# A decoder layer on one core: the feed-forward's first product as seven half-size products per block

## The chip, the core and the metric

The kernel runs on one core of a Trainium2 chip. Its time is the device time of one execution in microseconds (us), the median of several runs. The core has TensorE (matmuls; PE in the rows, PEld for its weight loads), VectorE (DVE), ScalarE (ACT), GpSimd (POOL) and SyncE (SP, which here only issues DMAs). Each engine works off its own queue in order. Matmuls write to PSUM, eight banks of 128 x 512 float32; everything else lies in SBUF.

## What is computed

One layer of a decoder on 512 tokens with 1024 features: a mixer with three groups of heads, then a feed-forward, each between two norms. The change touches the feed-forward:

```python
h = rmsnorm(x, pre_ffn_g[l])
gate, up = jnp.split(h @ w_ffn_in[l], 2, axis=-1)
f = (jax.nn.silu(gate) * up) @ w_ffn_out[l]            # 2816 -> 1024
x = x + rmsnorm(f, post_ffn_g[l])
```

All arrays are float32. D_FF is 2816, which is 22 blocks of 128.

## The kernel before

Every float32 operand of a large product is split into a high part (`h`, rounded to float32r by ScalarE) and a low part (`l`, the rest, by VectorE or GpSimd), and a product is three float32r matmuls: high x high, high x low, low x high. Weights arrive by DMA in pieces of 512 KB into the tile `wf` (pool `wpool`, two buffers); `Feed.split` (lines 174 to 186) makes `wh` (line 183, ScalarE) and `wl` (line 185, VectorE, or GpSimd where `on_pool` says so) from them. All matmuls are issued on line 112, transposes on line 117, weight loads by DMA on line 156.

The stages that matter here, in order:

- The mixer's output product (`tm_gemm`, two halves of 512 features). Its second half goes token tile by token tile; behind each tile come the epilogue (lines 1113 to 1132) and `turn` (lines 1141 to 1162): the norm, transposes of the tile to channels-first into the banks `rb` and `yb`, and the split into `h2` (line 1158, ScalarE) and `l2` (line 1159, VectorE), both 128 x 8 x 512.
- The first product of the feed-forward (lines 1171 to 1209). Blocks 0 and 1 are taken in two token halves of 256, so that the first half can start before the last tokens are turned: four weights (gate and up of two blocks), 24 matmuls of 256 columns each, then the second half. Blocks 2 to 21 follow with 512 columns: for gate and for up, eight slices of 128 features by three matmuls, 48 matmuls a block, in two banks `acc` or two banks `sb` in turn.
- `gate` (lines 1178 to 1183) of each block: silu on ScalarE into `etmp`, the product with up on VectorE, the high part (1182, ScalarE) and the low part (1183, VectorE).
- The second product (lines 1211 to 1219): `f_units`, pairs of blocks, each times 4 token tiles, in two halves of 512 features, with weights from `w_ffn_out` in the same manner.

The order of TensorE's instructions is written out by hand; `Order` (`od`) interleaves side work, such as the transposes of `turn`, by nominal times. For the other engines and their DMA queues a scheduler chooses the order when the kernel is built, by readiness in its own model and by priority; `tc.high_priority` raises it. An engine then executes that order as it stands. Synchronisation is derived from which tiles an instruction reads and writes.

SBUF is managed in pools on two stacks (`side="right"` is the second). A pool that is opened where a closed pool lay shares its memory. A pool opened with `reuse_waits="tile"` waits for the old tiles that it overlaps, one by one; without it the default "pool" holds. Line 1052 closes the pool `sol` (with the tile `y`) and line 1053 opens `early` there (`x2`, `grow`, `frow`); lines 1068 to 1072 close the mixer's pools and open `wsplit2` and `res`.

Of the kernel before, what the change touches and what calls it, by code (L numbers as in the profile page):

```python
# [96 lines left out]
def block_kernel(ctx: ExitStack, tc: tile.TileContext, x, pre_mix_g, w_in, rwkv_mu, rwkv_w0, rwkv_w2,  # L97
# [30 lines left out]
    def acc():  # L128
        return bank("acc", 2)
# [919 lines left out]
    for ui, unit in enumerate(o_units):  # L1049
        if ui == 2:  # L1050
            od.until("att2")
            sol.close()
            early = ph2.enter_context(tc.tile_pool(name="early", bufs=1, side="right"))
            x2 = early.tile([128, NB, D], F32, name="x2")
            grow = early.tile([128, D], F32, name="grow")
            frow = early.tile([128, D], F32, name="frow")
            act.dma_start(grow, brow(post_mix_g[0], D))
            act.dma_start(frow, brow(pre_ffn_g[0], D))
# [9 lines left out]
    ph1.close()  # L1068
    wsp2 = ph2.enter_context(tc.tile_pool(name="wsplit2", bufs=2, side="right"))


    res = ph2.enter_context(tc.tile_pool(name="res", bufs=1))
    wpools = (wspool, wsp2)
    h2 = res.tile([128, KB, S], F32R, name="h2")
    l2 = res.tile([128, KB, S], F32R, name="l2")
    sm = res.tile([128, 3 * NB], F32, name="sm")
    raw = res.tile([128, NB, 512], F32, name="raw")

    def tm_gemm(fd, ah, al, units, fin, by_token, banks, halves=(0, 1), parts=1):


        for hf in halves:
# [20 lines left out]
            for t in range(NB):  # L1103
                for part in range(len(pa[t])):
                    for ui in range(nun - tail, nun):
                        step(ui, t, part)

    def epilogue(gr, after):
        ys = {}

        def fin(t, p, a, b):
# [3 lines left out]
            if a == 0:  # L1115
                ys[t] = raw[:, t, :]
            elif a == 512:
                ys[t] = res.tile([128, 512], F32, name="etmp", bufs=2)
            dve.tensor_tensor(ys[t][:, a % 512:a % 512 + b - a], p, gr[:, a:b], op=OP.mult)  # L1119
# [21 lines left out]
    def turn(t):  # L1141
# [11 lines left out]
        for i in range(2):  # L1153
# [16 lines left out]

    FM = FB - KB
    fhm = res.tile([128, FM, S], F32R, name="fhm")
    flm = res.tile([128, FM, S], F32R, name="flm")
    fh = [fhm[:, i] if i < FM else mh[:, i - FM] for i in range(FB)]
    fl = [flm[:, i] if i < FM else ml[:, i - FM] for i in range(FB)]
    ffeed = Feed([(w_ffn_in[0], slice(0, 8), c + 128 * b, 128) for b in range(FB) for c in (0, FF)], wpools, on_pool=(1, 3))

    def gate(b, pg):
        f = res.tile([128, S], F32, name="etmp", bufs=2)
        act.activation(f, pg[0], AF.Silu)  # L1180
        dve.tensor_tensor(f, f, pg[1], op=OP.mult)
        act.copy(fh[b], f)
# [11 lines left out]

    ws = [ffn_w() for _ in range(4)]
# [5 lines left out]
    gate(0, pf[0:2])  # L1201
    gate(1, pf[2:4])
# [9 lines left out]
    orow = early.tile([128, D], F32, name="grow")  # L1212
    act.dma_start(orow, brow(post_ffn_g[0], D))
    wfeed = Feed([(w_ffn_out[0], pair_slice(k), 512 * hf, 512) for hf in range(2) for k in f_units], wpools)

# [34 lines left out]
```

## Time and profile before

| | us |
|---|---|
| median of 3 runs | 693.94 |
| lowest, highest | 693.78, 695.75 |
| the profiled execution, its own time | 693.72 |
| its span, first to last instruction | 692.0 |
| TensorE busy in it | 661.3 (96%) |
| VectorE, ScalarE, GpSimd busy | 335.6, 253.1, 137.0 |
| mean granted TensorE clock | 0.991 of full speed |

All rows come from that one profiled execution; times in them count from the span's start. The profiled end of a matmul is modelled, and matmuls overlap, so the pace of TensorE is read from starts of one matmul to starts of the next, not from durations.

### The profile page before, as it was taken

What the parts mean: (1) busy time and instruction counts of PE and PEld (TensorE: products, weight loads), DVE (VectorE), ACT (ScalarE), POOL (GpSimd) and SP (SyncE); (2) the same over time, 40 slices, a digit from 0 to 9 for tenths busy, and PEclk for the clock granted to TensorE, in tenths of its full rate; (3) what the DMA queues carried; (4) which work ended last, traced back from release to release, by engine and by line L of the source; (5) the groups of instructions that cost most, each with busy time, mean ns of one, the idle gap of its engine ahead of it and who ended that gap; (6) DMA issues with size and microseconds to landing.
All of it is one profiled execution on the core that took longest, in us unless ns stands there. A gap on an engine that the chain in (4) does not pass through costs nothing.

```text
span 692.0 us, 9733 instructions
## 1 busy us (share of the span) xinstructions
PE 661.3 (96%) x3918; PEld 542.8 (78%) x3918; DVE 335.6 (48%) x588; ACT 253.1 (37%) x451; POOL 137.0 (20%) x157
## 2 busy tenths in 40 slices
PE   7997999799999997997999999999999999999996
PEld 6876768677778885777988888888888888888885
DVE  4698879935354676358433233332323332222214
ACT  6753443435454463434422233222223221122111
POOL 6373447532423235115000000000000000000001
PEclk9999999899999999999999999999999999999999
DMA  7422112311212117225233333333333222323303
GB/s 234 121 62 62 33 38 82 92 32 37 50 31 60 33 55 251 94 59 152 68 116 101 105 99 92 91 92 95 109 100 91 92 91 92 94 99 101 99 4 122
DMA packets 80287, 61.15 MB, mean 88 GB/s; under 512 B 2121, under 2 KB 70129, under 8 KB 80241
## 3 DMA queue, kind: packets, MB, share of 16 engines
q1 hardware_dynamic: 78192, 57.70, 27.3%
q10 hardware_dynamic: 2048, 2.82, 1.4%
q8 instruction: 31, 0.51, 0.3%
q14 instruction: 16, 0.12, 0.1%
HBM read 58.41 MB, written 2.10 MB: 87 GB/s over the span
## 4 chain that ended last, share of the span: by engine, by line
PE 51%; DVE 2%; issue 1%; ACT 1%; POOL 1%; DVEq 0%; POOLq 0%; ACTq 0%
PE sb L112 21%; PE acc L112 21%; PE yb L112 3%; PE rb L112 3%; PE ob L112 2%; DVE x L1132 1%; DVE xs L1149 1%; ACT raw L1145 1%; POOL rs L1129 0%; POOL ss L1147 0%; DVE etmp L1119 0%; ACT wdad L1113 0%; DVE wl L185 0%; DVEq L1246 0%; PE rb L117 0%
## 5 line engine op out<-in xcount | busy, mean ns | idle before, releaser
L183 ACT ACTIVATE wh<-wf 128x1024 fp32r<-128x1024 f32 (+2 forms) x120 | 104.1, 886 | 285.4 <-PE sb L112 123.1
L185 DVE TENSOR_TENSOR wl<-wf,wh 128x1024 fp32r<-128x1024 f32 (+1 forms) x76 | 89.3, 1180 | 170.7 <-ACT wh L183 168.4
L185 POOL TENSOR_TENSOR wl<-wf,wh 128x512 fp32r<-128x512 f32 (+2 forms) x44 | 71.4, 1641 | 102.8 <-ACT wh L183 70.6
L1129 POOL TENSOR_TENSOR rs<-rs,mhalf 128x1 f32<-128x1 f32 x8 | 6.2, 778 | 379.9 <-DVE rs L1124 376.2
L112 PE MATMUL acc<-l,wh 128*128 128x512 f32 (+1 forms) x192 | 71.7, 374 | 1.9 <-DVE l L1159 1.9
L112 PE MATMUL sb<-l,wh 128*128 128x512 f32 (+1 forms) x192 | 71.6, 373 | 0.0
L112 PE MATMUL sb<-h,wh 128*128 128x512 f32 (+1 forms) x192 | 71.5, 373 | 0.0
L112 PE MATMUL acc<-h,wh 128*128 128x512 f32 (+1 forms) x192 | 71.5, 372 | 0.0
L112 PE MATMUL sb<-h,wl 128*128 128x512 f32 (+1 forms) x192 | 71.1, 371 | 0.0
L112 PE MATMUL acc<-h,wl 128*128 128x512 f32 (+1 forms) x192 | 71.1, 370 | 0.0
L112 PE MATMUL acc<-bigh,wh 128*128 128x512 f32 (+1 forms) x168 | 68.3, 410 | 0.7 <-ACT bigh L276 0.5
L112 PE MATMUL acc<-bigl,wh 128*128 128x512 f32 (+1 forms) x168 | 64.0, 386 | 0.3
L112 PE MATMUL acc<-bigh,wl 128*128 128x512 f32 (+1 forms) x168 | 59.5, 379 | 0.0
L112 PEld LDWEIGHTS acc<-l,wh 128*128 128x128 f32 x192 | 36.1, 188 | 8.3 <-DVE l L1159 2.2
L112 PEld LDWEIGHTS acc<-h,wh 128*128 128x128 f32 x192 | 36.1, 188 | 6.6
L112 PEld LDWEIGHTS sb<-h,wh 128*128 128x128 f32 x192 | 36.1, 188 | 6.6
L112 PEld LDWEIGHTS acc<-h,wl 128*128 128x128 f32 x192 | 36.1, 188 | 6.5
L112 PEld LDWEIGHTS sb<-h,wl 128*128 128x128 f32 x192 | 36.1, 188 | 6.5
L112 PEld LDWEIGHTS sb<-l,wh 128*128 128x128 f32 x192 | 36.1, 188 | 6.1
L112 PEld LDWEIGHTS acc<-bigh,wh 128*128 128x128 f32 x168 | 32.0, 191 | 8.6 <-issue 2.0
L112 PEld LDWEIGHTS acc<-bigl,wh 128*128 128x128 f32 x168 | 32.1, 191 | 5.8 <-DVE bigl L277 0.9
L112 PEld LDWEIGHTS acc<-bigh,wl 128*128 128x128 f32 x168 | 30.2, 191 | 6.3
(345 smaller groups left out, 1271.0 us busy)
## 6 DMA issues: line engine op xcount, KB each, us to landing
wf<-in_w_ffn_in_dram SPq DMA_DIRECT2D x44, 512.0 KB
wf<-in_w_ffn_out_dram SPq DMA_DIRECT2D x22, 512.0 KB
wf<-in_w_in_dram SPq DMA_DIRECT2D x21, 512.0 KB
wf<-in_w_out_dram SPq DMA_DIRECT2D x8, 512.0 KB
xt<-in_x_dram SPq DMA_DIRECT2D x4, 512.0 KB
x<-in_x_dram SPq DMA_DIRECT2D x4, 512.0 KB
out_dram<-x SPq DMA_DIRECT2D x8, 256.0 KB
wf<-in_w_in_dram SPq DMA_DIRECT2D x4, 384.0 KB
```

Source lines behind the costliest of these rows:

```text
L112: return nc.tensor.matmul(out_, lhsT, rhs, **kw)
L183: act.activation(h[:, c], t[:, c], AF.Copy)
L185: eng.tensor_tensor(l[:, c], t[:, c], h[:, c].bitcast(F32), op=OP.subtract)
L1129: pool.tensor_tensor(r, r, mhalf[:, 0:1], op=OP.pow)
L1132: dve.scalar_tensor_tensor(x2[:, t, c:d], src, r, x2[:, t, c:d], op0=OP.mult, op1=OP.add)
L1145: act.activation(raw[:, t, :].bitcast(BF), x2[:, t, :], AF.Square, scale=1.0 / 32, accum_out=ss[:, t:t + 1])
L1149: dve.scalar_tensor_tensor(xs, x2[:, t, :], ss[:, t:t + 1], frow, op0=OP.mult, op1=OP.mult)
```

## The change

Blocks 0 and 1 of the first product stay as they were. For blocks 2 to 21 the product of the 256 x 1024 weights (gate and up, 128 columns each) with the 1024 x 512 tokens is cut in two in each direction: weights into a11, a12 (gate, features 0 to 511 and 512 to 1023) and a21, a22 (up), tokens into b11, b12, b21, b22 (features by token halves). Seven products of the half size replace eight, as in Strassen's method in Winograd's form: four sums of weights (s1 to s4) and four of tokens (t1 to t4) go in, and the results are combined afterwards.

- Sums of tokens: `turn` also writes `ht`, a float32 copy of the turned tokens (one more ScalarE copy per bank). VectorE forms t1 to t4 there once (four operations of 1024 elements), and each is split into high and low parts; t1 takes the place of the original quarter in `h2`, `l2`.
- Sums of weights, per block (`weights`): SP loads a21 into half of `sa`, a11 into half of `sc`, a11 and a12 into `g` (pool `wpool`), a22. GpSimd's queue then issues two accumulating loads of 256 KB: a22 is added onto a21 in `sa` (s1), a21 onto a11 in `sc` (s3). VectorE forms s2 = s1 + a11 into the other half of `sa` and s4 = a12 + s2 into the other half of `sc`. All are split (`in_parts`): high parts on ScalarE, low parts on VectorE, none on GpSimd.
- Products: 84 matmuls of 256 columns a block, in the order a11 b11, s2 t2, s1 t1, a22 t4, s3 t3, s4 b22, a12 b21, into four banks (`acc` and three others, by turns). Three banks are accumulated onto a second time, after ScalarE or VectorE has read them in between.
- Combination: s1 and s5 (ScalarE), u2, u3, m, e (VectorE), one half of m on GpSimd, silu in two halves, then the product with `m`. Blocks 2 to 7 are split at once into the mixer's old tiles; blocks 8 to 21 are kept as float32 in `fr` and split after the last block, into tiles of the new pool `out`.
- Pools: `res` is divided. `normed` (h2, l2, the parts of t2 to t4) stays until the last block; `res` (raw, ht, t3, etmp, xs) is closed after the token sums and block 1's gate, and `ffn` (sa, sc, a22, all parts of 512 elements, every third wide one, the small tiles) is opened in its place with the default. `wsplit3` and `out`, opened after the last block, have `reuse_waits="tile"`.

```diff
@@ turn @@
-            act.copy(h2[:, 4 * i:4 * i + 4, tk], p3)
-            dve.tensor_tensor(l2[:, 4 * i:4 * i + 4, tk], p3, h2[:, 4 * i:4 * i + 4, tk].bitcast(F32), op=OP.subtract)
+            ks_ = slice(4 * i, 4 * i + 4)
+            act.copy(h2[:, ks_, tk], p3)
+            act.copy(ht[:, ks_, tk], p3)
+            dve.tensor_tensor(l2[:, ks_, tk], p3, h2[:, ks_, tk].bitcast(F32), op=OP.subtract)
@@ first product @@
-    for b in range(2, FB):
-        pg = []
-        for i in range(2):
-            p = (sb if b % 2 else acc)()
-            ffn_mm(p, *ffn_w(), slice(0, S))
-            pg.append(p)
-        gate(b, pg)
+    with tc.high_priority(offset=PRI_W):
+        dve.tensor_tensor(t3, b22, b12, op=OP.subtract)
+        dve.tensor_tensor(b12, b11, b12, op=OP.subtract)
+        dve.tensor_tensor(b22, b22, b12, op=OP.add)
+        dve.tensor_tensor(b21, b21, b22, op=OP.subtract)
+        act.activation(th_[:, 0], b22, AF.Copy, scale=-1.0)
+        dve.scalar_tensor_tensor(tl_[:, 0], b22, -1.0, th_[:, 0].bitcast(F32), op0=OP.mult, op1=OP.subtract)
+        for src, h, l in ((b12, quarter(h2, 0, 1), quarter(l2, 0, 1)),
+                          (b21, th_[:, 2], tl_[:, 2]), (t3, th_[:, 1], tl_[:, 1])):
+            act.copy(h, src)
+            dve.tensor_tensor(l, src, h.bitcast(F32), op=OP.subtract)
...
+    trans.close()
+    more.close()
+    gains.close()
+    ffs = ExitStack()
+    fr = ph2.enter_context(tc.tile_pool(name="inner", bufs=1, side="right")).tile([128, FB - FM, S], F32, name="fr")
+    fp_ = ffs.enter_context(tc.tile_pool(name="ffn", bufs=1))
...
+    def load(t, k, c0, add=False):
+        t = t.rearrange("p (k c) -> p k c", c=128)
+        if add:
+            pool.dma_start(t, w_rows[:, k:k + t.shape[1], c0:c0 + 128], accum_op=OP.add)
+        else:
+            sp.dma_start(t, w_rows[:, k:k + t.shape[1], c0:c0 + 128])
+
+    def in_parts(src, eng):
+        h, l = parts(src.shape[1])
+        act.activation(h, src, AF.Copy)
+        eng.tensor_tensor(l, src, h.bitcast(F32), op=OP.subtract)
...
+    def weights(b):
+        cg, cu = 128 * b, FF + 128 * b
+        sa = fp_.tile([128, 1024], F32, name="sa", bufs=2)
+        sc = fp_.tile([128, 1024], F32, name="sc", bufs=2)
+        g = wpool.tile([128, 1024], F32, name="wf")
+        a22 = fp_.tile([128, 512], F32, name="a22", bufs=2)
+        load(sa[:, 512:], 0, cu)
+        load(sc[:, :512], 0, cg)
+        load(g, 0, cg)
+        load(sa[:, 512:], 4, cu, add=True)
+        load(sc[:, :512], 0, cu, add=True)
+        load(a22, 4, cu)
+        a11, a12 = g[:, :512], g[:, 512:]
+        w = {}
+        w["a11"], = in_parts(a11, dve)
+        dve.tensor_tensor(sa[:, :512], sa[:, 512:], a11, op=OP.add)
+        w["s2"], w["s1"] = in_parts(sa, dve)
+        w["a22"], = in_parts(a22, dve)
+        dve.tensor_tensor(sc[:, 512:], a12, sa[:, :512], op=OP.add)
+        w["s3"], w["s4"] = in_parts(sc, dve)
+        w["a12"], = in_parts(a12, dve)
+        return w
+
+    def product(p, w, x, first=True):
+        (wh, wl), (xh, xl) = w, BT[x]
+        p = p[:, :256]
+        for k in range(4):
+            pe.matmul(p, wh[:, k], xh[:, k], start=(first and k == 0), stop=False, skip_group_check=True)
+            pe.matmul(p, wh[:, k], xl[:, k], start=False, stop=False, skip_group_check=True)
+            pe.matmul(p, wl[:, k], xh[:, k], start=False, stop=(k == 3), skip_group_check=True)
...
+    for b in range(NPLAIN, FB):
+        with tc.high_priority(offset=PRI_W):
+            w = weights(b)
+        pa, (pb, pc, pd) = acc(), ((sb(), sb(), sb()) if b % 2 else (rb(), yb(), ob()))
...
+        product(pa, w["a11"], "b11")
+        with tc.high_priority(offset=2 * PRI_W):
+            act.copy(s1, qa)
+        product(pb, w["s2"], "t2")
+        with tc.high_priority(offset=2 * PRI_W):
+            dve.tensor_tensor(u2, qb, s1, op=OP.add)
+        product(pc, w["s1"], "t1")
+        with tc.high_priority(offset=2 * PRI_W):
+            act.activation(s5, qc, AF.Copy, scale=-1.0)
+        product(pd, w["a22"], "t4")
+        product(pb, w["s3"], "t3", first=False)
+        with tc.high_priority(offset=2 * PRI_W):
+            dve.tensor_tensor(u3, qb, s1, op=OP.add)
+            dve.tensor_tensor(m[:, 0:256], qd, u3, op=OP.subtract)
+            pool.tensor_tensor(m[:, 256:512], s5, u3, op=OP.subtract)
+        product(pc, w["s4"], "b22", first=False)
+        with tc.high_priority(offset=2 * PRI_W):
+            dve.tensor_tensor(e[:, 256:512], qc, u2, op=OP.add)
+            act.activation(e[:, 256:512], e[:, 256:512], AF.Silu)
+        product(pa, w["a12"], "b21", first=False)
+        with tc.high_priority(offset=2 * PRI_W):
+            act.activation(e[:, 0:256], qa, AF.Silu)
+        if b < FM:
+            dve.tensor_tensor(e, e, m, op=OP.mult)
+            to_parts(b, e)
+        else:
+            dve.tensor_tensor(fr[:, b - FM], e, m, op=OP.mult)
+    ffs.close()
+    hps.close()
+    wsp2 = ph2.enter_context(tc.tile_pool(name="wsplit3", bufs=2, reuse_waits="tile"))
+    fo = ph2.enter_context(tc.tile_pool(name="out", bufs=1, reuse_waits="tile"))
...
+    for b in range(FM, FB):
+        fh.append(fhm[:, b - FM])
+        fl.append(flm[:, b - FM])
+        act.copy(fh[b], fr[:, b - FM])
+        dve.tensor_tensor(fl[b], fr[:, b - FM], fh[b].bitcast(F32), op=OP.subtract)
```

## Rows read from the trace of the kernel before

**Rows 1.** The page: busy us, share of the span and instructions of each engine.

```profile
PE 661.3 (96%) x3918; PEld 542.8 (78%) x3918; DVE 335.6 (48%) x588; ACT 253.1 (37%) x451; POOL 137.0 (20%) x157
```

**Rows 2.** Chain in order of time, 340 to 365 us: start, us, what.

```profile
343.86 10.96 PE acc L112 x48
```

**Rows 3.** Busy us by stretch: engines with instruction counts, PEclk, DMA share, GB/s.

```profile
400.00:450.00 50.00, 50.00 (x221) 41.25 (x220) 17.47 (x19) 14.28 (x19) 0.00 (x0) 1.00 0.33 95
```

**Rows 4.** Single matmuls in time: start, duration, engine, line, out<-in, shapes.

```profile
332.51 0.28 PE L112 MATMUL acc<-h,wh 128*128 128x256 f32 x1
...
335.38 0.28 PE L112 MATMUL acc<-h,wh 128*128 128x256 f32 x1
...
337.99 0.28 PE L112 MATMUL acc<-h,wl 128*128 128x256 f32 x1
338.10 0.28 PE L112 MATMUL sb<-h,wh 128*128 128x256 f32 x1
...
343.70 0.40 PE L112 MATMUL acc<-h,wh 128*128 128x512 f32 x1
...
562.39 0.40 PE L112 MATMUL rb<-wh,fhm 128*128 128x512 f32 x1
```

**Rows 5.** VectorE: groups (busy us, mean ns | idle before), then two in time.

```profile
L185 DVE TENSOR_TENSOR wl<-wf,wh 128x1024 fp32r<-128x1024 f32 x68 | 83.3, 1225 | 168.2 <-ACT wh L183 165.9
L1183 DVE TENSOR_TENSOR flm<-etmp,fhm 128x512 fp32r<-128x512 f32 x14 | 9.6, 686 | 0.0
L796 DVE TENSOR_TENSOR y<-y,sb 128x256 f32<-128x256 f32 x6 | 2.5, 418 | 0.1
...
339.46 1.22 DVE L185 TENSOR_TENSOR wl<-wf,wh 128x1024 fp32r<-128x1024 f32 x1 [0.26 <-ACT wh L183]
340.60 0.68 DVE L1183 TENSOR_TENSOR flm<-etmp,fhm 128x512 fp32r<-128x512 f32 x1
```

**Rows 6.** ScalarE: groups of the weight splits, columns as in rows 5.

```profile
L183 ACT ACTIVATE wh<-wf 128x1024 fp32r<-128x1024 f32 x74 | 78.5, 1061 | 253.2 <-PE sb L112 123.1 <-PE acc L112 85.8 <-PE yb L112 31.2
L183 ACT ACTIVATE wh<-wf 128x512 fp32r<-128x512 f32 x38 | 21.9, 623 | 25.0 <-PE acc L112 23.7 <-DMA wf<-in_w_in_dram 0.7 <-issue 0.4
```

**Rows 7.** GpSimd and VectorE side by side in time (merged rows have a count).

```profile
261.42 9.78 POOL L185 TENSOR_TENSOR wl<-wf,wh 128x1024 fp32r<-128x1024 f32 x2 [3.32 <-ACT wh L183]
...
313.22 2.42 POOL L185 TENSOR_TENSOR wl<-wf,wh 128x1024 fp32r<-128x1024 f32 x1
313.29 2.90 DVE L1132 SCALAR_TENSOR_TENSOR x<-raw,rs,x 128x512 f32<-128x512 f32 x1 [0.43 <-POOL rs L1129]
```

**Rows 8.** A weight load's issue on SP's queue and the ScalarE split it released.

```profile
337.86 3.22 SPq L156 DMA_DIRECT2D wf<-in_w_ffn_in_dram  x2
...
341.90 1.06 ACT L183 ACTIVATE wh<-wf 128x1024 fp32r<-128x1024 f32 x1 [1.97 <-DMA wf<-in_w_ffn_in_dram]
```

**Rows 9.** The last reads of y (pool sol), the first loads into pool early.

```profile
257.88 1.89 DVE L802 TENSOR_TENSOR bigl<-y,bigh 128x512 fp32r<-128x512 f32 x3
...
259.80 1.53 SPq L1066 DMA_DIRECT2D x<-in_x_dram  x3
259.80 0.35 ACTq L1057 DMA_DIRECT2D grow<-in_post_mix_g_dram  x1
```

**Rows 10.** TensorE's wait for a low part, and the last low part.

```profile
317.51 0.39 PE L112 MATMUL acc<-l,wh 128*128 128x256 f32 x1 [1.88 <-DVE l L1159]
...
330.67 0.68 DVE L1159 TENSOR_TENSOR l<-yb,h 128x512 fp32r<-128x512 f32 x1
```

**Rows 11.** Block 1's gate on VectorE.

```profile
344.13 0.68 DVE L1181 TENSOR_TENSOR etmp<-etmp,sb 128x512 f32<-128x512 f32 x1
...
346.93 0.68 DVE L1183 TENSOR_TENSOR flm<-etmp,fhm 128x512 fp32r<-128x512 f32 x1
```

**Rows 12.** Busy us by stretch around TensorE's idle time, columns as in rows 3.

```profile
130.00:132.70 2.70, 0.00 (x0) 0.00 (x0) 2.63 (x4) 0.00 (x0) 0.40 (x1) 1.00 0.37 106
132.70:134.20 1.50, 1.46 (x49) 1.39 (x49) 1.50 (x1) 0.00 (x0) 0.61 (x2) 0.51 0.53 159
...
138.00:140.00 2.00, 2.00 (x15) 1.26 (x16) 0.56 (x1) 0.00 (x1) 0.92 (x2) 0.61 0.00 0
```

More of the change, by code (lines that the diff above doesn't have):

```diff
@@ L1054, in block_kernel @@
             x2 = early.tile([128, NB, D], F32, name="x2")
-            grow = early.tile([128, D], F32, name="grow")
-            frow = early.tile([128, D], F32, name="frow")
+            gains = ExitStack()
+            gfp = gains.enter_context(tc.tile_pool(name="gains", bufs=1, side="right"))
+            grow = gfp.tile([128, D], F32, name="grow")
+            frow = gfp.tile([128, D], F32, name="frow")
             act.dma_start(grow, brow(post_mix_g[0], D))
@@ L1106, in tm_gemm @@
                         step(ui, t, part)
+    pools = {"tmp": res, "raw": raw}
     def epilogue(gr, after):
         ys = {}
+        raw = pools["raw"]
         def fin(t, p, a, b):
@@ L1117, in fin @@
             elif a == 512:
-                ys[t] = res.tile([128, 512], F32, name="etmp", bufs=2)
+                ys[t] = pools["tmp"].tile([128, 512], F32, name="etmp", bufs=2)
             dve.tensor_tensor(ys[t][:, a % 512:a % 512 + b - a], p, gr[:, a:b], op=OP.mult)
@@ L1168, in block_kernel, with to_parts @@
     tm_gemm(ofeed, mhk, mlk, o_units, ofin, 4, {1: (sb, sb, sb, ob)}, (1,))
[L1171 to L1181, printed above, removed]
+    FM = KB
+    NPLAIN = 2
+    fh = [mh[:, i] for i in range(FM)]
+    fl = [ml[:, i] for i in range(FM)]
+    ffeed = Feed([(w_ffn_in[0], slice(0, 8), c + 128 * b, 128) for b in range(NPLAIN) for c in (0, FF)], wpools,
+                 on_pool=(1, 3))
+    def to_parts(b, f):
         act.copy(fh[b], f)
@@ L1193, in ffn_w @@
         return tuple(w.rearrange("p (k c) -> p k c", k=KB) for w in ffeed.next())
-    ws = [ffn_w() for _ in range(4)]
+    ws = [ffn_w() for _ in range(2 * NPLAIN)]
     pf = [acc(), acc(), sb(), sb()]
@@ L1200, in block_kernel @@
             ffn_mm(p, *w, slice(256 * th, 256 * th + 256))
-    gate(0, pf[0:2])
-    gate(1, pf[2:4])
-    for b in range(2, FB):
-        pg = []
-        for i in range(2):
-            p = (sb if b % 2 else acc)()
-            ffn_mm(p, *ffn_w(), slice(0, S))
-            pg.append(p)
-        gate(b, pg)
+    for b in range(NPLAIN):
+        f = res.tile([128, S], F32, name="etmp", bufs=2)
+        act.activation(f, pf[2 * b], AF.Silu)
+        dve.tensor_tensor(f, f, pf[2 * b + 1], op=OP.mult)
+        to_parts(b, f)
@@ new lines, in block_kernel, with quarter @@
+    K_ = [slice(0, 4), slice(4, 8)]
+    TK = [slice(0, 256), slice(256, 512)]
+    def quarter(t, k, tk):
+        return t[:, K_[k], TK[tk]]
+    b11, b12, b21, b22 = [quarter(ht, k, t) for k in range(2) for t in range(2)]
+    with tc.high_priority(offset=PRI_W):
[9 more added lines that the diff above has]
+            dve.tensor_tensor(l, src, h.bitcast(F32), op=OP.subtract)
@@ new lines, in block_kernel, with parts @@
+    fp_ = ffs.enter_context(tc.tile_pool(name="ffn", bufs=1))
+    n_wide = [0]
+    def parts(n):
+        if n == 512:
+            return tuple(fp_.tile([128, 512], F32R, name=x, bufs=3) for x in ("sh", "sl"))
+        n_wide[0] += 1
+        po = fp_ if n_wide[0] % 3 == 0 else wspool
+        return tuple(po.tile([128, 1024], F32R, name=x) for x in ("wh", "wl"))
+    w_rows = w_ffn_in[0].rearrange("(k p) c -> p k c", p=128)
+    def load(t, k, c0, add=False):
[4 more added lines that the diff above has]
+            sp.dma_start(t, w_rows[:, k:k + t.shape[1], c0:c0 + 128])
@@ new lines, in product, with small @@
+    def product(p, w, x, first=True):
[5 more added lines that the diff above has]
+            pe.matmul(p, wl[:, k], xh[:, k], start=False, stop=(k == 3), skip_group_check=True)
+    def small(name):
+        return fp_.tile([128, 256], F32, name=name)
@@ L1214, in block_kernel @@
+    flm = fo.tile([128, FB - FM, S], F32R, name="flm")
+    for b in range(FM, FB):
[3 more added lines that the diff above has]
+        dve.tensor_tensor(fl[b], fr[:, b - FM], fh[b].bitcast(F32), op=OP.subtract)
     wfeed = Feed([(w_ffn_out[0], pair_slice(k), 512 * hf, 512) for hf in range(2) for k in f_units], wpools)
```

33 lines of the change are left out of this document (27 added, 6 removed).

## The prediction

> **What bounds the kernel now.** I read the page's busy shares first, then the chain that ended last in order of time, then busy time by stretch, then single instructions. TensorE is busy 96% of the span [rows 1], and through the feed-forward's first product the chain is nothing but its matmuls, some 10.95 us for each group of 48 [rows 2]. In 400 to 450 us TensorE is busy all 50, VectorE 17.5, ScalarE 14.3, GpSimd 0, and the DMA engines a third of the time at 95 GB/s [rows 3]. So in this stage TensorE alone sets the pace and the others have room; fewer TensorE columns are time won, as long as what prepares them fits into the room.
>
> The stage is delimited by three starts: the first half of the second group of tokens ends and block 2 begins at 343.70, the second product at 562.39 [rows 4]. Blocks 2 to 21 thus take 218.7 us, 10.93 each, or 0.228 per 512-column matmul (48 a block).
>
> **What the change takes from TensorE.** A block becomes seven products of 4 x 3 matmuls, 84 of 256 columns. The trace has that form: the two plain blocks run in token halves, and 48 of them take 343.70 - 338.10 = 5.60 us, 0.1167 each with a fresh weight load every time [rows 4]. 84 x 0.1167 = 9.80 us a block, 196.0 for 20: **22.7 us less**. Of seven eighths one would expect 27.3; the rest goes because two half matmuls cost 0.233, not 0.228. The rate is not quite one number: 24 matmuls from 332.51 to 335.38 go at 0.120, the 23 after them to 337.99 at 0.1135 [rows 4]; at these ends the gain is 17 or 28 us.
>
> **What it adds per block, beside TensorE.** VectorE: five operations of 512 elements, two of 1024, four of 256 that read PSUM, and a multiply (blocks 2 to 7 also a subtract) of 512. Durations are 0.69, 1.23 and 0.42 us; the next operation starts about 0.08 before the profiled end (1.14 after a start where the duration is 1.22) [rows 5], so 5 x 0.61 + 2 x 1.14 + 4 x 0.34 + 2 x 0.61 = 7.9 us, and 7.3 from block 8 on. GpSimd's one 256-element operation can hold VectorE for its length: a 512-element VectorE operation took 2.90 us instead of some 0.7 while GpSimd's 1024-element one of 2.42 ran [rows 7]; a quarter of that is 0.6. So 8.5 of 9.8 us. ScalarE: three of 0.62 and two of 1.06 [rows 6] plus five small ones, some 6 us. Both hide under TensorE, with 13% left on VectorE; it executes in order, and u2 must be added before TensorE may accumulate onto its bank, two products (2.8 us) later. In the six heavy blocks, begun with no lead, I take 0.3 us of stall each, **+1.8 us**; zero is the low end (the rate above already holds the floor, so no gain), 1.0 on six blocks the high end. DMA: five plain pieces of 256 KB instead of four, and two that accumulate. Plain transfers now fill a third of the time at 95 GB/s [rows 3], i.e. 290 GB/s when busy, 0.9 us per 256 KB: 4.5 us, and the accumulating two 1.8 (as plain) to 3.6 (reading their target too), 6.3 to 8.1 of 9.8 us. Each tile has two buffers, so loads run a block or more ahead.
>
> **The hand-over into the new form** is where I look for the loss. The new pool ("ffn") lies where the pool "res" was, which is closed after the second plain block's gate; the new pool has no tile-wise reuse. What a closed pool does shows at 259.8: the loads of x2 and of grow, two tiles of a new pool, are issued together 0.03 us after the last read of y, a tile of the closed pool [rows 9]. So the loads of sa, sc and a22, and even the split of a11, wait until the last reader of res, the subtract of block 1's gate. PE's last plain matmul is at 343.7. From there:
> - gate and token-sum split: in the trace that subtract ends at 346.93 + 0.68, 3.9 after [rows 11], with a weight split between that is no longer there; bare (0.69 + 0.62 + 0.68 and pipeline) 2.3. I take 3.0.
> - the 256 KB load of sa: a 512 KB load issued at 337.86 released ScalarE at 341.90, 4.0 us [rows 8], 1.8 of it transfer; so 3.1 (at most 4.0).
> - the accumulating load behind it, issued from GpSimd's queue, where the trace has none. Low end 3.1, as a plain load. High end 8.9: 4.9 of GpSimd's work (what its 1024-element operations took when they met VectorE, 9.78 for two [rows 7]), 2.2 fixed, 1.8 for two-fold data. I take 5.3: 3.1 + 0.9 for reading the target + 1.3 for GpSimd's part, nearer the low end because these bytes pass no GpSimd lane.
> - sum 0.69, high part 1.06, low part 1.23, hand-overs 0.1: 3.1 [rows 5, 6].
> That is 14.5 us until the second product can start; the first (1.4 us, needs only a11) runs inside it: TensorE idles 13.1 us. After an idle of 4.0 us before 132.74 the granted clock is at its lower level (0.51, 1.2 of 2.4 GHz) from 132.7 and 0.61 on average in 138 to 140, so at half until about 139.6: of 6.9 us half is lost, 3.4 [rows 12]. I take 3.0 (1.5 to 3.4). Hand-over: **+16.1 us**, between 11.7 and 22.2.
>
> The Trainium skill (DMA: Bandwidth & Descriptors, Anatomy of one DMA) gives a DMA from GpSimd 2.0 us plus its bytes at 436 GB/s, 2.6 us for 256 KB as an estimate; with it the hand-over would be 2.7 us shorter and the time 687.2. No run here shows such a DMA yet.
>
> **The rest.** The turn to channels-first gets eight more ScalarE copies (0.62 each at most) between the high parts; TensorE waits there already for the low part, 1.88 us at 317.51 [rows 10], so the copy ahead adds up to 0.5 twice: **+0.8 us** (0 to 1.2). The four token sums and three splits fit between 331.35, the end of the last low part [rows 10], and 343.7: some 10 us of VectorE; the fourth split waits for the last plain matmuls on its tokens and is in the 3.0 above. At the end, the 14 conversions of blocks 8 to 21 (8.5 us of VectorE) are needed only by the fifth unit of the second product, 22 us after its start, the second unit's weights (in a pool that reuses tile by tile) after 5.6; both have time: **0**. If that cover failed, a weight split of 2.3 us would show.
>
> Sum against the profiled execution: 693.72 - 22.7 + 1.8 + 16.1 + 0.8 = 689.7; that execution lies 0.2 under the median of the runs, 693.94: **689.9 us**. Of its own, this case reaches from 683 to 699.
>
> **Rivals.**
> - No gap at the hand-over: if loads could land before the gate is through. 689.9 - 16.1 = **674 us**. For: g and the first wide split use older pools. Against: rows 9, and that sa, sc, a22 lie on tiles read until after 343.7. Chance 0.12.
> - Accumulating loads set the pace, on GpSimd's queue: two of them and the 256-element operation per block. At 4.9 us each [rows 7] a block takes 10.5, and the first one is 3.6 later: 689.9 - 1.8 + 20 x 0.7 + 3.6 = **706 us**. It is slower than before from 10.1 us a block, i.e. 4.7 per accumulating load. For: VectorE reads SBUF nearly all the time, and GpSimd's operations doubled beside it. Against: 2.5 to 3 us each, as the loads in the trace suggest, leaves a third free. Chance 0.20. The Trainium skill speaks against this change here (SBUF — State Buffer, Who interferes with whom): a DMA issued by GpSimd can be starved of descriptors by VectorE, and it advises a hardware queue; but the same section excepts tensor_tensor, which is all VectorE does in a block. By the first half the rival's 706 would follow, by the second not; no row here decides.
> - VectorE sets the pace: in-order waits for ScalarE's high parts, which each low part needs, bring a block to 10.3: 689.9 - 1.8 + 10 = **698 us**. Against: 8.5 of 9.8 by rows. Chance 0.07.
> - The change doesn't do what it says: 256-column matmuls with changing operands at 0.130 a piece give 10.92 a block, no gain, 693.9 + 16.1 + 0.8 + 1.8 = **712 us**. Against: rows 4. Chance 0.03.
>
> **How the numbers follow.** Forecast 0.58 (689.9). A measurement can tell about 0.3%, 2.1 us, from no change. Of the forecast's 0.58, 0.38 lies below 691.9, 0.13 within, 0.07 above 696.0; the first rival is all faster, the second and fourth slower, the third 0.02 same and 0.05 slower. Faster 0.50, same 0.15, slower 0.35. The range 680 to 709 leaves out the first rival (0.12) and the upper part of the second and fourth.
>
> **What would show it.** Right: matmuls of 256 columns at 0.117 in unbroken rows, blocks of 9.8 us; one TensorE gap of some 13 us before the second product of block 2, ended by the low part of sa, with the clock at half behind it; SP's loads of sa issued right after block 1's last subtract. Wrong: loads of sa issued before 344 (first rival); GpSimd waiting or working through whole blocks and VectorE's sums released by accumulating loads (second); TensorE released by VectorE in every block with VectorE over 95% (third).

## The result and the profile after

| | before | changed |
|---|---|---|
| median, us | 694.85 (4 runs) | 722.42 (4 runs, 719.94 to 724.25) |
| ratio | 1 | 1.039, 95% interval 1.037 to 1.041 |
| profiled execution: span, us | 692.0 | 718.2 |
| last matmul of the plain blocks 0 and 1 starts, us | 343.59 | 343.38 |
| second product starts, us | 562.39 | 589.80 |
| from there to the end of the span, us | 129.6 | 128.4 |

The change costs 27.6 us, outside the predicted range, and all of it lies in the stage that was changed: from the last plain matmul to the second product it took 246.4 us instead of 218.8. The page of the changed kernel, busy time of each engine and then the DMA queues with packets, MB and share of the engines' time (compare rows 1):

```profile
PE 657.7 (92%) x4638; PEld 575.3 (80%) x4638; DVE 432.5 (60%) x776; ACT 305.4 (43%) x583; POOL 203.4 (28%) x217
...
q1 hardware_dynamic: 89072, 62.94, 29.2%
q0 software_dynamic: 21120, 10.49, 11.8%
```

TensorE is busy about as long as before, though it does an eighth less of the product; VectorE is at 60%. q0 is new: the accumulating loads. Busy time by stretch, as in rows 3; 410 to 420 is one of three stretches in which the granted clock falls:

```profile
410.00:420.00 10.00, 7.71 (x52) 7.51 (x51) 6.33 (x11) 5.42 (x10) 3.21 (x3) 0.83 0.86 175
430.00:500.00 70.00, 66.77 (x546) 65.56 (x546) 49.00 (x80) 30.80 (x58) 20.62 (x19) 1.00 0.80 166
```

Beside TensorE nothing is full in the longer stretch: VectorE has 49 of 70 us, GpSimd 21, the DMA engines 80%. TensorE nevertheless stops. Its starts around one stop (start, duration, what, and in brackets the idle time before it and what ended that):

```profile
411.35 0.28 PE L112 MATMUL ob<-th,sl 128*128 128x256 f32 x1
413.91 0.58 PE L112 MATMUL rb<-th,wh 128*128 128x256 f32 x1 [2.29 <-DVE u L1325]
414.29 0.42 PE L112 MATMUL rb<-tl,wh 128*128 128x256 f32 x1
```

It is ready for the fifth product, which accumulates onto the bank that u2 is read from, and VectorE has not added u2 yet. Fifteen blocks have such a stop of 0.2 to 2.6 us, and after three of them the granted clock is at its lower level for some 3 to 4 us (0.83 on average in 410 to 420). Why VectorE is late is told by the list of waits, 360 to 590 us (total us, times, longest), and by VectorE's and then SP's instructions in time:

```profile
DVE sa L1292 <- DMA wf<-in_w_ffn_in_dram: 67.0, 17, 5.4
```

```profile
445.04 0.68 DVE L1272 TENSOR_TENSOR sl<-wf,sh 128x512 fp32r<-128x512 f32 x1
...
446.85 0.41 DVE L1325 TENSOR_TENSOR u<-sb,s 128x256 f32<-128x256 f32 x1
451.20 0.69 DVE L1292 TENSOR_TENSOR sa<-sa,wf 128x512 f32<-128x512 f32 x1 [3.94 <-DMA wf<-in_w_ffn_in_dram]
...
455.28 1.26 DVE L1272 TENSOR_TENSOR wl<-sa,wh 128x1024 fp32r<-128x1024 f32 x1
456.46 0.68 DVE L1272 TENSOR_TENSOR sl<-wf,sh 128x512 fp32r<-128x512 f32 x1
...
458.26 0.41 DVE L1325 TENSOR_TENSOR u<-rb,s 128x256 f32<-128x256 f32 x1
```

```profile
445.75 0.37 SPq L1267 DMA_DIRECT2D wf<-in_w_ffn_in_dram  x1
...
456.56 0.37 SPq L1267 DMA_DIRECT2D sa<-in_w_ffn_in_dram  x1
457.16 0.37 SPq L1267 DMA_DIRECT2D wf<-in_w_ffn_in_dram  x1
```

This is a loop. SP can issue the load of `wf` for a block only when VectorE has made the low part of a12 of two blocks earlier, the last reader of that buffer (445.04 + 0.68, issue at 445.75). The load lands 5.45 us later, and VectorE goes on at 451.20. The sum that waits for it, s2 (line 1292), stands in VectorE's fixed order ahead of the low part of a12 of the block before (456.46), and that one frees the buffer for the next load (issue at 457.16): 5.96 us of VectorE's work. 5.45 + 5.96 = 11.4 us a block, whatever TensorE needs. The second term is 5.96 or 5.97 us in 15 of 16 blocks; the first is 4.6 to 6.9 us, 5.7 on average over the 17 waits. While VectorE stands before the sum (3.94 us here), everything behind it stands too, the next u2 (458.26) among it.

The loop has a second leg of almost the same length. In SP's queue a load of `sa` stands 0.6 us ahead of that of `wf`; it is issued (456.56) when the low part of the wide split of `sa` is done (455.28 + 1.26), and that one stands behind s2 too.

### The profile page after: what moved, and what is told of

It reads as the page before. It is cut to its first block, busy times and chain, and to the rows that moved or that the text cites. A ratio compares the mean times of both kernels' runs of the same rounds, so it can differ in the third digit from the quotient of the medians.

```text
span 718.2 us, 11832 instructions
## 1 busy us (share of the span) xinstructions
PE 657.7 (92%) x4638; PEld 575.3 (80%) x4638; DVE 432.5 (60%) x776; ACT 305.4 (43%) x583; POOL 203.4 (28%) x217
## 3 DMA queue, kind: packets, MB, share of 16 engines
q0 software_dynamic: 21120, 10.49, 11.8%
## 5 line engine op out<-in xcount | busy, mean ns | idle before, releaser
L183 ACT ACTIVATE wh<-wf 128x512 fp32r<-128x512 f32 (+2 forms) x80 | 61.5, 798 | 118.3 <-PE sb L112 34.4
L185 DVE TENSOR_TENSOR wl<-wf,wh 128x1024 fp32r<-128x1024 f32 (+1 forms) x36 | 40.3, 1131 | 77.7 <-ACT wh L183 77.5
L112 PE MATMUL acc<-h,sh 128*128 128x256 f32 x160 | 46.1, 288 | 3.6 <-ACT sh L1271 3.6
L112 PE MATMUL acc<-h,sl 128*128 128x256 f32 x160 | 46.0, 287 | 0.0
L112 PE MATMUL acc<-l,sh 128*128 128x256 f32 x160 | 45.9, 287 | 0.0
L1265 POOL DMA_DIRECT2D sa<-in_w_ffn_in_dram x20 | 26.3, 1313 | 68.6 <-DMA sa<-in_w_ffn_in_dram 45.1
L1334 POOL TENSOR_TENSOR m<-s,u 128x256 f32<-128x256 f32 x20 | 14.7, 735 | 106.2 <-DVE u L1332 106.2
L112 PE MATMUL rb<-th,wh 128*128 128x256 f32 x80 | 24.6, 308 | 17.8 <-DVE u L1325 10.1
L112 PEld LDWEIGHTS acc<-h,sh 128*128 128x128 f32 x160 | 31.4, 196 | 3.8 <-ACT sh L1271 3.8
L1265 POOL DMA_DIRECT2D sc<-in_w_ffn_in_dram x20 | 27.4, 1372 | 20.1 <-DMA sc<-in_w_ffn_in_dram 18.7
L112 PE MATMUL sb<-h,wh 128*128 128x256 f32 x112 | 32.6, 291 | 0.0
```

The source lines that it names most:

```text
L112: return nc.tensor.matmul(out_, lhsT, rhs, **kw)
L183: act.activation(h[:, c], t[:, c], AF.Copy)
L185: eng.tensor_tensor(l[:, c], t[:, c], h[:, c].bitcast(F32), op=OP.subtract)
L1265: pool.dma_start(t, w_rows[:, k:k + t.shape[1], c0:c0 + 128], accum_op=OP.add)
L1334: pool.tensor_tensor(m[:, 256:512], s5, u3, op=OP.subtract)
```

## Experiments

All but e4 start from the changed kernel; e4 starts from the kernel before. The stage is counted from the start of the last plain matmul to the start of the second product of the feed-forward, the hand-over from the same start to the first matmul of block 2's second half-size product (s2 t2); both in the profiled execution. The kernel before ran beside each of them; its medians there were 695.0 to 695.4. Line numbers are those of each kernel's own file.

| kernel | median us | ratio to before, interval | stage | hand-over |
|---|---|---|---|---|
| before | 695 | | 218.8 | |
| changed | 722.4 | 1.037 to 1.041 | 246.4 | 14.8 |
| e1, late sum | 696.2 | 0.998 to 1.003 | 219.7 | 15.6 |
| e2, no accumulating loads | 688.4 | 0.983 to 0.993 | 212.6 | 8.1 |
| e3, tile-wise reuse | 713.9 | 1.021 to 1.031 | 234.7 | 9.4 |
| e4, before in halves | 700.3 | 1.004 to 1.008 | 224.1 | |
| e5, e1 and e3 | 692.9 | 0.994 to 0.998 | 218.0 | 9.7 |
| e6, e1 and 64 bytes | 692.8 | 0.995 to 0.999 | 219.2 | 15.2 |
| e7, e1 and 128 bytes | 698.3 | 1.003 to 1.009 | 223.2 | 15.6 |
| e8, e5 and another layout | 693.0 | 0.996 to 1.000 | 219.3 | 10.6 |
| e13, e5, m on VectorE | 686.9 | 0.983 to 0.991 | 212.8 | 9.4 |
| e10, e5, all sums on VectorE | 686.4 | 0.987 to 0.991 | 213.1 | 8.1 |
| e11, e10 and a layout | 688.0 | 0.989 to 0.993 | 212.6 | 8.1 |
| e12, e11 and 64 bytes | 676.9 | 0.972 to 0.976 | 201.8 | 8.1 |

### Is it the loop, or the accumulating loads themselves?

The theory is the loop; the first rival is that two accumulating loads a block, or the DMA engines, set the pace. e1's edit moves s2 in VectorE's order, behind the multiply of two blocks before, and nothing else; SP's order follows from it:

```diff
-        dve.tensor_tensor(sa[:, :512], sa[:, 512:], a11, op=OP.add)
+        with (tc.issue_after(mults[b - 2].ins) if b - 2 in mults else ExitStack()):
+            dve.tensor_tensor(sa[:, :512], sa[:, 512:], a11, op=OP.add)
...
-            dve.tensor_tensor(fr[:, b - FM], e, m, op=OP.mult)
+            mults[b] = dve.tensor_tensor(fr[:, b - FM], e, m, op=OP.mult)
```

> The VectorE sum that forms sa of a block (it waits for the load of wf) is issued behind the multiply of two blocks before, instead of between that block's u2 and u3; nothing else is changed. Theory (a loop over wf's two buffers: the load lands some 5.4 us after its buffer is free, VectorE's fixed order then needs some 6 us until it frees the next): VectorE's waits for wf, 67 us in 17 blocks, fall below 15 us, blocks go from 11.4 to 10.1-10.4 us, TensorE's gaps before the fifth product and the stretches at the lower clock behind them vanish, 693 to 700 us in all. Rival 1 (the two accumulating loads, or the DMA engines at 75 to 84% of their time, set the pace): blocks stay at 11.2 us or more, the waits only change their place, 716 to 724 us. Rival 2 (VectorE's own work with its in-order waits): the waits move to another VectorE instruction, 705 to 716 us.

696.2 us: 26 us back, as the theory had it. The wait for `wf` is gone from VectorE's list, and TensorE is busy through (stretch of e1, then the load of `wf` and the sum that needs it):

```profile
430.00:500.00 70.00, 69.71 (x581) 69.51 (x580) 53.91 (x84) 35.89 (x63) 23.18 (x21) 1.00 0.89 184
```

```profile
433.72 0.37 SPq L1268 DMA_DIRECT2D wf<-in_w_ffn_in_dram  x1
```

```profile
445.37 0.69 DVE L1294 TENSOR_TENSOR sa<-sa,wf 128x512 f32<-128x512 f32 x1
```

581 matmuls in the time of 546, at a DMA share of 0.89: the accumulating loads do not bound it at this pace. The load of `wf`, issued at 433.72, now has 11.6 us until its sum at 445.37, instead of 5.45; both legs of the loop are open, for SP now issues it ahead of that of `sa` (438.39). e2 keeps VectorE's order and SP's and drops the accumulating loads:

```diff
-        load(sa[:, 512:], 4, cu, add=True)
-        load(sc[:, :512], 0, cu, add=True)
```

> Leaves out the two accumulating loads of every block, so two of the four weight sums lack one term; all VectorE, ScalarE and TensorE work is as in the changed kernel. Theory (loop over wf's two buffers, its length the landing time of wf's load plus some 6 us): without the accumulating traffic wf lands after about 4 us instead of 5.4, blocks are 10.1 to 10.4 us, and the hand-over loses the accumulating load of some 5 us: 690 to 697 us. Rival (accumulating loads set the pace by themselves): blocks fall to the TensorE time of 10.08, with 688 to 693 us; the two differ by the landing time of wf and by whether VectorE still waits for it. If VectorE's order alone were the cause, independent of any load, 714 us or more remain.

688.4 us. By the number alone this is the rival's range (688 to 693) and 1.6 us under the theory's; e1, where the accumulating loads stay and TensorE runs through, speaks against the rival, and so does the trace of e2: VectorE still waits for `wf` once a block, yet TensorE does not stop, since the loop is shorter:

```profile
430.00:500.00 70.00, 70.00 (x585) 70.00 (x585) 50.77 (x83) 34.39 (x62) 5.17 (x7) 1.00 0.46 132
```

```profile
453.74 0.69 DVE L1290 TENSOR_TENSOR sa<-sa,wf 128x512 f32<-128x512 f32 x1 [2.59 <-DMA wf<-in_w_ffn_in_dram]
```

```profile
449.64 0.37 SPq L1267 DMA_DIRECT2D wf<-in_w_ffn_in_dram  x1
...
459.69 0.37 SPq L1267 DMA_DIRECT2D wf<-in_w_ffn_in_dram  x1
```

449.64 to 453.74 is 4.10 us of landing, 453.74 to 459.69 again 5.95 of VectorE: 10.05. Over the 18 waits of e2 the landing is 4.3 us on average and the sum 10.2, about TensorE's 10.08. So both were needed for the loss, the order and a load that lands some 1.4 us later beside the accumulating traffic (5.7 against 4.3); each undone alone removes it. A third buffer of `wf` was not tried. The pool "ffn" leaves no room for it, and with SP's queue as it stands it would hardly have been enough, since the load of `sa` ahead of that of `wf` waits for VectorE behind s2 as well.

### The hand-over

```diff
-    fp_ = ffs.enter_context(tc.tile_pool(name="ffn", bufs=1))
+    fp_ = ffs.enter_context(tc.tile_pool(name="ffn", bufs=1, reuse_waits="tile"))
```

> The new pool takes over its space tile by tile instead of as a whole. Theory of the hand-over (loads wait for the last reader of the closed pool): those of the loads whose space is read earlier come earlier; the accumulating load stays behind its plain one. The gap of TensorE at block 2, some 11.8 us with 3.5 lost to the clock, shrinks by 3 to 10 us, 712 to 719 us in all, the pace of 11.4 us a block unchanged. Rival (the tiles lie on what the second plain block's gate reads last anyway): no change, 721 to 724 us.

713.9 us, 8.5 less; its runs scatter from 709.5 to 716.3. In the profiled one, the fastest, the stage is 11.8 us shorter: 5.4 at the hand-over, the rest in the steady part. There the loop and 59 us of waits for `wf` remain, but the loads land after 5.2 us on average instead of 5.7, and one stretch at the lower clock is left of three; why was not looked into. In e3 `sa` is loaded at 327.25 and its accumulating load issued at 330.80, both long before the gate; what is late next is the load of `sc`, which lies on `ht`, at 345.91, and behind it in SP's queue that of a22.

e5 is e1 and e3 together:

> The late sum and the tile-wise reuse of the new pool together. If the two costs are separate (a pace of 11.4 us a block from the loop over wf, and a wait of the first loads for the whole closed pool), their gains add: 696.2 less the 8.5 us that tile-wise reuse alone brought, 686 to 690 us, with blocks of 10.1 us and gaps of about 3 and 4 us at block 2. If they are one cost seen twice, 693 to 697 us remain.

692.9 us, above the 686 to 690 of the theory that the gains add: against e1 the reuse gave 3.3, not 8.5. The hand-over is 5.9 shorter, but in every third block TensorE now stops for u2 again. The engines around one such stop in e5, GpSimd first:

```profile
440.04 1.28 POOL L1266 DMA_DIRECT2D sa<-in_w_ffn_in_dram  x1 [7.58 <-DVE sl L1273]
440.81 1.27 POOL L1336 TENSOR_TENSOR m<-s,u 128x256 f32<-128x256 f32 x1
```

```profile
442.11 0.69 DVE L1348 TENSOR_TENSOR fr<-e,m 128x512 f32<-128x512 f32 x1 [2.14 <-POOL m L1336]
442.72 0.69 DVE L1294 TENSOR_TENSOR sa<-sa,wf 128x512 f32<-128x512 f32 x1
...
444.53 0.42 DVE L1327 TENSOR_TENSOR u<-rb,s 128x256 f32<-128x256 f32 x1
```

```profile
445.00 0.39 PE L112 MATMUL rb<-th,wh 128*128 128x256 f32 x1 [0.55 <-DVE u L1327]
```

GpSimd's half of m could run from 437.3 on, after u3 (436.85 + 0.42); it stands behind an accumulating load that waits until 440.04, and the multiply, the late sum and u2 wait for it one after the other. What the load waits for is the plain load of `sa` that it adds onto, issued at 435.23: 13 of 16 such waits are put down to that, and the `sl` named in this row ends in the same 0.1 us. e13 moves that half of m to VectorE and keeps the accumulating loads:

```diff
-            pool.tensor_tensor(m[:, 256:512], s5, u3, op=OP.subtract)
+            dve.tensor_tensor(m[:, 256:512], s5, u3, op=OP.subtract)
```

> Both changes (late sum, tile-wise reuse), accumulating loads kept, and the 256-element subtract of m moved from GpSimd to VectorE. Theory for the small gaps that are left with both changes (0.4 to 1.2 us before the fifth product in every third block): the subtract stands in GpSimd's queue behind an accumulating load that waits, the multiply waits for it, the late sum is issued behind the multiply, and u2 behind the sum. Then the gaps go with the move, 4 to 6 us: 687 to 690 us. Rival (the nearly full DMA engines land something late): the gaps stay, 691 to 695 us.

686.9 us, no stop in any block, with the DMA share still at 0.89 in 430 to 500. So the small stops came from GpSimd's queue and not from full DMA engines.

e8 is e5 with another order of the new pool's tiles: they are allocated ahead of their use, the late ones on `ht`:

```diff
...
+    fp_.tile([128, 1024], F32R, name="wh"), fp_.tile([128, 1024], F32R, name="wl")
+    for n in ("s1", "u2", "u3", "s5"):
+        fp_.tile([128, 256], F32, name=n)
...
```

> The late sum and tile-wise reuse, with the new pool's tiles in another order: those that block 2 needs first (sa, sc, a22, sl) lie on tiles of the closed pool that are read for the last time before 335 us, those that are needed late (e, m, the small ones, the third wide split) on ht, which is read until 346. Theory (loads stand in SP's queue behind the load of sc, which waits for ht): all of block 2's loads are issued before 335, the gap before the second product falls from 3.8 us to below 1, TensorE does not fall to the lower clock, and 3 to 8 us are saved against both changes together: 679 to 685 us. Rival (VectorE's splits and the gate of the plain blocks are what is late next): 685 to 690 us.

693.0 us, nothing won, where 679 to 685 was expected. `sc` was loaded early as meant (330.84), but the buffer of a22 that block 2 uses came to lie on `etmp`, and its load was issued at 348.01; the low part of a22 (351.75) stands ahead of the sum (353.56) in VectorE's order.

### What the accumulating loads buy

Their second operands are in SBUF anyway: a22 in its own tile, a21 and a11 in `sa` and `wf`. e10 forms all four sums on VectorE and saves the load of `sc` as well:

```diff
-        load(sc[:, :512], 0, cg)
...
-        load(sa[:, 512:], 4, cu, add=True)
-        load(sc[:, :512], 0, cu, add=True)
...
+        with (tc.issue_after(mults[b - 2].ins) if b - 2 in mults else ExitStack()):
+            dve.tensor_tensor(sc[:, :512], sa[:, 512:], a11, op=OP.add)
+        dve.tensor_tensor(sa[:, 512:], sa[:, 512:], a22, op=OP.add)
```

> Late sum and tile-wise reuse, and the two accumulating loads replaced by two more VectorE sums of 512 elements from pieces that are in SBUF anyway (sa's and a22's loads, wf), so the plain load of sc goes too. The DMA engines' share falls from 0.88 to below 0.4 in these blocks, VectorE gets 1.2 us a block more, some 8.8 of 10.1. Theory (with the late sum TensorE's own 10.08 us a block is the bound, and the small gaps that are left, 5 us in all, come from full DMA engines): 685 to 690 us. Rival 1 (the accumulating loads were worth their price because VectorE has no room): TensorE waits for VectorE in every block, 700 us or more. Rival 2 (neither limits): as both changes together, 691 to 695.

686.4 us, 6.5 less than e5. VectorE has the room (64.4 of 70 us), and the DMA share falls from 0.89 to 0.36 (stretch of e10):

```profile
430.00:500.00 70.00, 70.00 (x586) 70.00 (x585) 64.35 (x98) 35.18 (x63) 8.41 (x8) 1.00 0.36 105
```

So the accumulating loads bought nothing that was needed here; e13, which keeps them, is as fast. e11 then places the tiles of block 2 on space that is free early, a22 among them:

> As the run before it, with the new pool's tiles ordered so that sa, a22, and the parts sh and sl lie on space that is free before 335 us. Theory: the load of a22 no longer waits for the gate and for ht, VectorE's low part of it no longer stands before the sums for some 2.3 us, the gap before the second product falls from 4.5 us to 2 or less: 2 to 4 us less than the run before it. Rival (VectorE's order, gate first, is all that counts): within 1 us of it.

688.0 us, no gain, as the rival had it, and 1.6 us more than e10, which is beyond the rival's 1 us: a22 is now loaded at 329.38, but the hand-over stays at 8.1 us. In VectorE's order block 2's sums stand behind the second plain block's gate, whose last subtract starts at 348.86 in e11. Whether another order there would save the rest was not tried.

### The pace of a 256-column matmul

In blocks 2 to 21 the changed kernel's matmuls start every 0.120 us between stops, not every 0.1167 as forecast. e4 is the kernel before with its matmuls cut in halves of 256 columns:

```diff
-            ffn_mm(p, *ffn_w(), slice(0, S))
+            w = ffn_w()
+            for th in range(2):
+                ffn_mm(p, *w, slice(256 * th, 256 * th + 256))
```

> The kernel before, with the 48 matmuls of 512 columns of each of blocks 2 to 21 replaced by 96 of 256 columns (same work, twice the weight loads). By 0.1167 us each, the rate that I took from the plain blocks, a block takes 11.20 instead of 10.93: +5.4 us, 699 to 701. By 0.120, the rate that blocks 2 to 21 of the changed kernel show: 11.52, +11.8 us, 705 to 708. If 0.120 comes from something else in the changed kernel (its traffic, its tiles), 0.1135 to 0.1167 are seen here: 693 to 701.

700.3 us, ratio 1.006 (1.004 to 1.008). The mean is 0.1167 us, as forecast, but it is two paces: starts of the first gate weight's, the first up weight's and the next gate weight's matmuls, 48 each:

```profile
344.47 0.28 PE L112 MATMUL acc<-h,wh 128*128 128x256 f32 x1
...
350.23 0.28 PE L112 MATMUL acc<-h,wh 128*128 128x256 f32 x1
...
355.67 0.28 PE L112 MATMUL sb<-h,wh 128*128 128x256 f32 x1
```

5.76 / 48 = 0.1200 for the gate's and 5.44 / 48 = 0.1133 for the up's, and so on in the blocks behind. They differ in the place of their weights, in the pools "wsplit" and "wsplit2". The addresses that the kernel gives these tiles (bytes in a partition) are 60448 and 188384, that of `h2` 76832; modulo 128 they are 32, 96 and 32. In the changed kernel `h2` (76896) and all parts of weights are at 96. e6 and e7 are e1 with the token tiles shifted, by 64 and by 128 bytes; in e6 a second 64 bytes keep the parts of weights in the new pool at 96:

```diff
     hp = hps.enter_context(tc.tile_pool(name="normed", bufs=1))
+    hp.tile([128, 16], F32, name="pad")
...
+    fp_.tile([128, 16], F32, name="pad")
...
```

> The late sum, and 64 bytes of padding ahead of the token tiles (h, l, th, tl), which shifts them against the weight parts by 64 bytes per partition; a second 64 bytes keeps the new pool's weight parts at the residue of the older pool's. Theory (from the halves run: 0.1133 us a matmul with weight parts in one pool, 0.1200 with those in the other, the same token tile): where the addresses of the two operands agree modulo 128 bytes, 256 columns take 0.1200 us, where they differ 0.1133. Then all 84 matmuls of a block go at 0.1133, 9.52 us a block, 11.2 us less in 20 blocks: 684 to 689 us, or 688 to 693 if the DMA engines, busy some 90% in these blocks, hold them at 9.8 or so. Rival (the pool or the rest of the traffic decides, not the residue): 0.1200 stays, 694 to 698 us.

> The control of the padding: the late sum, and 128 bytes ahead of the token tiles, so that every tile moves and the residues modulo 128 stay as they were. Residue theory: 0.1200 us a matmul and 693 to 699 us, as the late sum alone. If any shift, or the larger distance, is what matters: 0.1133 and 684 to 690 us.

Between stops, e6 goes at 16.00 / 140 = 0.114 us a matmul and e7 at 30.00 / 251 = 0.1195:

```profile
460.00:476.00 16.00, 16.00 (x140) 15.99 (x139) 11.17 (x19) 8.11 (x15) 6.62 (x6) 1.00 0.82 184
```

```profile
420.00:450.00 30.00, 30.00 (x251) 30.00 (x252) 22.39 (x37) 14.86 (x28) 9.96 (x9) 1.00 0.88 180
```

The residue decides the pace. The time of e6, 692.8, is only 3.4 under e1's, and e7's is 2 above it, because both have more of e5's small stops than e1: in e6 up to 1.4 us in a block, after VectorE has waited for GpSimd's half of m. That GpSimd's queue makes them, and not the DMA engines, is read from the trace here; e13 tested it at the slower pace only. e12 is e11 with the 64 bytes, so the accumulating loads are gone, and the faster pace is paid out:

> As the run before it, with the 64 bytes of padding that make the matmuls of 256 columns go at some 0.1147 instead of 0.1200 us: 84 x 0.0053 x 20 = 8.9 us less if TensorE is the bound, 675 to 682 us. If VectorE (8.8 us of work a block, 9.6 to do it in) comes to set the pace, TensorE's gaps before the fifth product come back and less than 3 us is won.

676.9 us, 18 us less than before the change (stretch of e12):

```profile
430.00:500.00 70.00, 70.00 (x621) 70.00 (x619) 67.06 (x102) 37.25 (x66) 10.01 (x8) 1.00 0.38 111
```

621 matmuls in 70 us, 0.113 each. VectorE is at 96%, so one would expect it to be the next bound.

## Why the prediction was wrong

**The bound.** That TensorE alone sets the pace and saved columns are time won held once the loop was gone: e1 takes 696.2 us, the forecast of 689.9 and the 5.6 us by which the pace below was mis-sized give 695.5, and e10, e12 and e13 beat the kernel before.

**The pace, 9.80 us a block [rows 4].** Mis-sized: 84 x 0.120 = 10.08, 201.6 us instead of 196.0. The mean of two paces was carried over to a kernel in which all operands are placed as for the slower one. Both were in the rows; the range held it, the sum did not.

**The stalls, +1.8 us.** This is the step that failed: "Each tile has two buffers, so loads run a block or more ahead." Two buffers put the load ahead only if the buffer is freed a block ahead, and it is freed by an instruction that stands behind the wait for the next load. The runs showed a loop of 11.4 us a block in its place: the landing of `wf`, 5.45, and 5.96 of VectorE's work from the sum that waits for it to the low part that frees the next buffer. The stage of 246.4 us less 201.6 of matmuls, and less the hand-over below, leaves 29 us; counted from the starts, the fifteen stops and what hangs on them make 23 us and the starts at the lower clock 6. VectorE was costed as a sum of durations, 8.5 us a block, and that was about right or high (7.8 in e1: 53.9 us of 70); its order, and the loads' place in it, were not followed through two blocks. The range took 1.0 us on six blocks as the high end, when there was no bound on the others.

**The DMA, 6.3 to 8.1 us a block.** Too low: 0.89 x 10.08 = 9.0 in e1. Without the accumulating loads (e2, 430 to 500) the share is 0.46 for five plain pieces, 0.9 us each as forecast; the two add 4.3, 2.2 each, not 0.9 to 1.8. Their landing in the changed kernel, the last number of each row:

```profile
sa<-in_w_ffn_in_dram POOLq DMA_DIRECT2D x20, 256.0 KB, 5.0
sc<-in_w_ffn_in_dram POOLq DMA_DIRECT2D x20, 256.0 KB, 6.8
```

The 5.3 that I took lies between. With the Trainium skill's fit (DMA: Bandwidth & Descriptors, Anatomy of one DMA) a DMA from GpSimd of this size was estimated at 2.6 us; the trace disagrees by a factor of 1.9 to 2.6. In e3 the first one, issued at 330.80 with the DMA engines nearly idle (share 0.03 in 330 to 332), still took 4.8 us.

**The hand-over, +16.1 us [rows 8, 9, 11, 12].** Right in its total, and its path is the one that was described. SP's load of `sa`, GpSimd's accumulating load, and TensorE, in the changed kernel:

```profile
346.63 0.37 SPq L1267 DMA_DIRECT2D sa<-in_w_ffn_in_dram  x1
```

```profile
350.35 1.48 POOL L1265 DMA_DIRECT2D sa<-in_w_ffn_in_dram  x1 [23.50 <-PE acc L112]
```

```profile
347.27 0.58 PE L112 MATMUL acc<-h,sh 128*128 128x256 f32 x1 [3.61 <-ACT sh L1271]
...
358.21 0.58 PE L112 MATMUL rb<-th,wh 128*128 128x256 f32 x1 [7.71 <-ACT wh L1271]
```

(The matmul named in GpSimd's row had long been done; the accumulating load waits for the plain one.) Counted from 343.5, where a next plain matmul would have started, the gate is through after 3.1 us (3.0 forecast), the plain load takes 3.7 (3.1), the accumulating one 6.0 to the sum at 356.38 (5.3), sum and high part 1.8; my 3.1 held the low part too, for which TensorE waits only behind its first two matmuls, 0.47. The second product starts 14.7 us after 343.5; 14.5 was forecast. That this is so close is partly luck: the loads were taken 1.3 us too short and the path behind them 1.3 too long. With 1.44 of product 1 inside it and some 2.5 lost to the lower clock and the low part behind it, it cost 15.8 against 16.1. The upper bound of 22.2 adds up from its own terms to 21.9; nothing hangs on it.

**The turn, +0.8, and the end, 0.** The last plain matmul starts 0.2 us earlier than before, so the copies cost nothing that shows. The end is 1.2 us shorter; its matmuls on `fhm` start every 0.227 us instead of every 0.233.

**The rivals.** The highest number, 712 for matmuls at 0.130 us, came nearest, by luck: between stops they start every 0.120. Accumulating loads as the pace (706) had a part in the loss, and by another way than its own: neither GpSimd's queue nor their own duration bound the changed kernel, but the 1.4 us that they add to a plain load inside a loop. GpSimd's queue did matter, in e5, by what stood behind it. VectorE as the pace (698) had the right witness, TensorE released by VectorE, but VectorE was idle 30% of the time, not full. The sign of the first (674), loads of `sa` before 344, did not come: 346.63. That is the default's doing and not, as the prediction argued, the place of `sa`: with tile-wise reuse (e3) its load goes out at 327.25, so its space is free long before 343.7. The prediction named for each tile who reads it last at the hand-over, and did not ask the same in the steady state.

**The Trainium skill's rule against the change** (SBUF — State Buffer, Who interferes with whom: descriptors of GpSimd's DMAs starved by VectorE, tensor_tensor excepted). The first accumulating load took 6.0 us though VectorE was idle for the first half of it (until 353.33); later ones into `sa` took 5.0 at the median, beside a VectorE that is busy 70%. There is no sign of starvation, as by the second half of that rule.

## What to carry to other kernels

For each buffer that is refilled in a steady loop, write down which instruction frees it, how long the refill takes, and which instruction waits for the refill; if the waiting one stands ahead of the freeing one on the same engine, landing time plus the work between them is a lower bound of the period, however idle every engine looks. Look for the same in the queue that issues the refill: a load that stands ahead of it there and waits for the same engine closes the loop a second time. A sum of busy times bounds the pace only from below. An operation on an engine that also issues waiting DMAs inherits their waits (e5 against e13: 6 us), so a short one on a long chain is better off elsewhere.

## What the runs showed of the hardware beside that

- A matmul of 256 float32r columns starts every 0.1200 us where the addresses of its two operands agree modulo 128 bytes, and every 0.113 to 0.114 where they differ by 64 (e4, e6, e12; a shift by 128 bytes leaves it at 0.1195, e7). Other residues were not tried. At 512 columns it is not the same: in blocks 2 to 21 of the kernel before, the gate's matmuls, with weights and tokens both at 32, start every 0.2267 us and the up's, with weights at 96, every 0.229. In the changed kernel's second product they start every 0.2267 us with both operands at 96 (619.49 to 624.93, 24 of them) and every 0.2333 with one at 0 (597.27 to 602.87); but in the second product before, half of the matmuls on `fhm` have both operands at 96 too and start every 0.232. So the residue is not the whole of it there, and why is open.
- The granted clock does not follow the length of a stop alone. In the changed kernel it was at half (1.2 of 2.4 GHz) from the first matmul on after a stop of 2.29 us (before 413.91), and 0.50 from 517 to 519 after one of 1.90 us (before 515.09); after one of 2.55 us it stayed at full speed (0.39 against 0.58 us for the first matmul):

```profile
551.13 0.39 PE L112 MATMUL rb<-th,wh 128*128 128x256 f32 x1 [2.55 <-DVE u L1325]
```
